# GDN's chunk chain: both scan directions in one operation, its scratch in step order, its output stored from ScalarE's queue

## The chip, the cores and the metric

The kernel runs on one core of one Trainium2 chip. The metric is the device time of one execution in microseconds (us), the median of the runs shown. The engines are named as the profile names them: PE (TensorE's matmuls; PEld is its weight load), DVE (VectorE), ACT (ScalarE), POOL (GpSimd) and SP (SyncE, which here only issues DMAs). Each engine works through its own instructions in order.

## The reference

One layer of a diffusion backbone over 2048 latent tokens with 256 context tokens in front and a model width of 1024: modulated RMS norms, one input projection split among three mixers (gated DeltaNet, RG-LRU, RWKV-7), one output projection, and a squared-ReLU MLP of width 4096. The mixers scan in both directions. The change is in the gated DeltaNet (GDN): 6 heads of width 64, chunks of 64 tokens, so 36 chunk steps in each direction, the context's 4 chunks first.

```python
# per direction and head, chunk by chunk (C = 64)
L    = strict_lower((k*beta) @ k.T * decay)
u, w = solve(L + I, [v*beta, k*beta*exp(gc)])
attn = (q @ k.T) * decay
def step(S, xs):
    v_new = u_c - w_c @ S
    o     = qg_c @ S + a_c @ v_new
    S     = S * exp(gl_c) + kd_c.T @ v_new
# forward and backward: context first, then the latents; the two outputs are added
```

## The kernel before

The program has four stages. The front projects RWKV's columns and prepares its features. `mixed` runs RWKV's chunk chain and, woven into it, `gdn_features`: GDN's projection, convolution and norms, and from them the scratch arrays in DRAM (`kq` for keys and queries, `kv` for keys and values by rows, `dm` for the decay matrices, `gc` for per-row factors). `rest` runs GDN's chunk chain and, woven into it, everything else before the MLP: the LRU's projection and scans, GDN's gate, and, behind them, the output projection `out_proj`. The MLP (`ffn`) comes last.

GDN's chain in `rest` has four parts, each written for one direction `dd` and called for both in turn:

- `gram(dd, n)` loads the keys and the decay matrix of a chunk, multiplies the decay by beta on POOL, forms three pairs of 64x64 Gram matrices on PE and writes the product into `mu` on DVE. Up to 32 such units fill a round.
- `Lanes.invert` inverts a round of 64x64 triangular matrices at once: 30 pairs of multiply and add on DVE, with transposes around them and small matmuls (`lmc`, `lmy`) behind. There are 7 rounds.
- `load(dd, n)` loads a chunk's operands, forms `q @ k.T` on PE and multiplies it by the decay (`qa`, two operations of 64 partitions on DVE), scales queries and keys by the row decays on POOL (`qa`, `kqe`) and the keys by rows on ACT (`kv`, three operations).
- `step(dd, n)` is the recurrence: PE, then `r` on DVE; PE, then `s<-gps,colt` (two halves) on DVE; PE, then the new state `s<-se,gps` (two halves) on DVE; then the output on PE, its copy on ACT and its store `go<-o` from SP's queue. POOL decays the old state (`se`) beside it.

`chains` writes them out step by step, with Gram matrices up to 10 steps ahead of the chain and loads one step ahead. `weave` gives the other work (`others`) a number of turns for each turn of the chain: 1.0 at first, 0.7 once `out_proj` has begun. A stage of `out_proj` may begin once the chain has passed the chunks that it reads; its first one waits for step 23 to be over. From the order in which it is written, a scheduler sets the order on each engine.

The DMAs that SP issues take turns on eight completion semaphores, so that an issue also stands until the DMA eight places before it has landed.

The lines of the steps below are L1267 (`gram`), L1284 (`load`), L1323 (`step`), L463 (`backwards`) and L1531 (`rest`).

Of the kernel before, what the change touches and what calls it, by code (L numbers as in the profile page):

```python
# [43 lines left out]
def poff(p):  # L44
# [10 lines left out]
    "kq": ([2, 128, NCH, 2, 3, 64], F32),  # L55
    "kv": ([2, 128, NCH, 2, 192], F32),
# [3 lines left out]
    "gc": ([128, NCH, 18], F32),  # L60
    "dm": ([2, 128, NCH, 3, 64], F32),
# [8 lines left out]
    "go": ([2, 128, NCH - 4, 3, 64], F32),  # L70
# [392 lines left out]
def backwards(k, rows, turn=False):  # L463


    if not turn:
        to, src = [rows(i).rearrange("(a t) c x -> a t (c x)", t=64) for i in (1, 0)]
        k.S.dma_start(out=to, in_=src[:, ::-1, :])
        return
    for c in range(4):  # L470
        to, src = [rows(i)[:, j].rearrange("(a t) x -> a t x", t=64) for i, j in ((1, 3 - c), (0, c))]
        k.S.dma_start(out=to, in_=src[:, ::-1, :])


def gdn_features(k, es, sm):
# [9 lines left out]
    def rows(p, y, a):  # L485
        to_rows(k, sm, w, d["kv"][0, :, 4 * p:4 * p + 4, a, :], y, "gsq")

    def normed(p, y, sq, s):

        scale = 64.0 if s else 1.0  # L490
        k.table("natural_log_exp_and_others")
        for a, b in ((0, 2), (2, 3)):
            ps = sm.tile([128, 2, 256], F32, name="gssq", tag="sm")
            for j in range(a, b):
                k.mm(ps[:, j - a, :], k.ones2, sq[:, j, :])
            k.act(sq[:, a:b, :], ps[:, 0:b - a, :], AF.Ln, scale=scale, bias=scale * 1e-6)
# [15 lines left out]
    for s, p, h in pj.passes([tiles(GW) + [(C_BA, 24)], tiles(0), tiles(2 * GW)]):  # L512
# [118 lines left out]
def gates(k):  # L631


    d, tc, V, A, G = k.d, k.tc, k.V, k.A, k.G
# [74 lines left out]
def decays(k, pp):  # L709
# [13 lines left out]
    for p in range(NP):  # L723
# [8 lines left out]
        cols = w.tile([128, 4, 18], F32, name="cols", bufs=2)  # L732
        for par in range(2):
            V.tensor_copy(cols[HALF[par]], ps[HALF[par], :, 32 * par:32 * par + 18])
        k.S.dma_start(out=d["gc"][:, 4 * p:4 * p + 4], in_=cols)
        yield
        for dd in range(2):
# [4 lines left out]
            col = cols[:, :, 3 * dd:3 * dd + 3].rearrange("p c r -> p r c")  # L742
# [6 lines left out]
            k.S.dma_start(out=d["dm"][dd, :, 4 * p:4 * p + 4], in_=e)  # L749
# [11 lines left out]
def rwkv_sweep(k, pj, pss, beside):  # L761
# [4 lines left out]
    with ExitStack() as es:  # L766
# [41 lines left out]
        for i, p in enumerate(RW_ORDER):  # L808
# [41 lines left out]
            backwards(k, vr, True)  # L850
# [242 lines left out]
def chunk_of(dd, n):  # L1093

    b, i = divmod(n, 4)
    return 4 * piece_of(dd, b) + (i if dd == 0 else 3 - i)


# [150 lines left out]
def gdn_mixer(k, es, ln):  # L1249
    rounds = Rounds([24] + 6 * [32])  # L1250
# [3 lines left out]
    colt = c1.tile([128, NCH, 18], F32, name="colt")  # L1254
# [4 lines left out]
    w = es.enter_context(tc.tile_pool(name="gmw", bufs=3, side="right"))  # L1259
    ch = es.enter_context(tc.tile_pool(name="gch", bufs=2, side="right"))  # L1260
# [5 lines left out]
    ee, late = {}, {}  # L1266

    def gram(dd, n):
        c = chunk_of(dd, n)
        kq = ld.tile([128, 3, 64], F32, name="kq")  # L1270
        dm = ld.tile([128, 3, 64], F32, name="dm", bufs=3)
        k.S.dma_start(out=kq, in_=d["kq"][dd, :, c, 0])
        k.S.dma_start(out=dm, in_=d["dm"][dd, :, c])
        k.tt(G, dm, dm, colt[:, c, 12 + 3 * dd:15 + 3 * dd].unsqueeze(2).to_broadcast([128, 3, 64]), MUL)
        ps = psg.tile([128, 3, 64], F32, name="gg")
        for r in range(3):
            for par in range(2):
                k.mm(ps[half[1 - par], r, :], kq[half[par], r, :], kq[half[par], r, :])
        for q, u, r, end in rounds.runs(6 * n + 3 * dd, 3):
            k.stt(mu[:, u, :], ps[:, r, :], -1.0, dm[:, r, :], MUL, MUL)  # L1280
            yield q if end else None

    def load(dd, n):
        c = chunk_of(dd, n)  # L1284
        sl = c % 2
        if n % 2 == 0:

            e = w.tile([128, 3, 128], F32, name="e")
            t = 128 * (c // 2)
            for par in range(2):  # L1290
                src = d["gb"][3, dd, par::2, t:t + 128].unsqueeze(0).to_broadcast([64, 3, 128])
                k.S.dma_start(out=e[half[par]], in_=src)
            ee[dd] = e
        e = ee[dd][:, :, 64 * sl:64 * sl + 64]
        kq = ld.tile([128, 2, 3, 64], F32, name="kqe", bufs=4)
        qa = ld.tile([128, 2, 3, 64], F32, name="qa", bufs=4)
        kv = ld.tile([128, 2, 3, 64], F32, name="kv", bufs=4)
        kn, vn = kv[:, 0], kv[:, 1]
        dm = ld.tile([128, 3, 64], F32, name="dml", bufs=2)
        k.S.dma_start(out=kq, in_=d["kq"][dd, :, c])  # L1300
        k.S.dma_start(out=dm, in_=d["dm"][dd, :, c])
        k.S.dma_start(out=kv, in_=d["kv"][dd, :, c].rearrange("p a (r x) -> p a r x", x=64))
        ps = psc.tile([128, 3, 64], F32, name="gps")
        for r in range(3):
            for par in range(2):
                k.mm(ps[half[1 - par], r, :], kq[half[par], 0, r, :], kq[half[par], 1, r, :])
# [5 lines left out]
        for r in range(3):  # L1312
            k.act(kn[:, r, :], kn[:, r, :], AF.Copy, scale=colt[:, c, 6 + 3 * dd + r:7 + 3 * dd + r])
        late[dd, n] = (kq, qa, vn, kn, e[:, :, 63:64])


    st = []
    for dd in range(2):
        s = ch.tile([128, 2, 3, 64], F32, name=f"s{dd}")
        G.memset(s, 0.0)  # L1320
        st.append(s)

    def step(dd, n):  # L1323
        kq, qa, vn, kn, el = late.pop((dd, n))
        c = chunk_of(dd, n)
        s, s2 = st[dd], ch.tile([128, 2, 3, 64], F32, name=f"s{dd}")
        st[dd] = s2
        z = psc.tile([128, 3, 64], F32, name="gps")
        for r in range(3):
            for par in range(2):  # L1330
                h, o = half[par], half[1 - par]
                k.mm(z[o, r, :], kq[h, 0, r, :], s[h, par, r, :])
        r_ = ch.tile([128, 3, 64], F32, name=f"r{dd}", bufs=1)
        k.tt(V, r_, vn, z, SUB)
        se = ch.tile([128, 3, 64], F32, name=f"se{dd}", bufs=1)
        for par in range(2):
            h = half[par]
            k.tt(G, se[h], s[h, par], el[h].to_broadcast([64, 3, 64]), MUL)
        yield
        v = psc.tile([128, 3, 64], F32, name="gps")  # L1340
        for r in range(3):
            for o in half:
                q, u = rounds.lane(dd, n, r)
                k.mm(v[o, r, :], ys[q % 2][o, u, :], r_[o, r, :])
        bt = colt[:, c, 12 + 3 * dd:15 + 3 * dd].unsqueeze(2).to_broadcast([128, 3, 64])
        for par in range(2):
            o = half[1 - par]
            k.tt(V, s[o, par], v[o], bt[o], MUL)
        yield
        ds = psc.tile([128, 3, 64], F32, name="gps")  # L1350
        for r in range(3):
            for par in range(2):
                h, o = half[par], half[1 - par]
                k.mm(ds[h, r, :], kn[o, r, :], s[o, par, r, :])
        for par in range(2):
            h = half[par]
            k.tt(V, s2[h, par], se[h], ds[h], ADD)
        yield
        if n >= 4:
            out = psl.tile([128, 3, 64], F32, name="gout", tag="lm")  # L1360
            for r in range(3):
                for par in range(2):
                    k.mm(out[half[par], r, :], s[:, par, r, :], qa[:, par, r, :])
            os = ch.tile([128, 3, 64], F32, name=f"o{dd}")
            A.copy(os[:, :, ::-1] if dd else os, out)
# [3 lines left out]
    def both(f):
        return lambda n: [f(dd, n) for dd in range(2)]  # L1370

    return chains(k, rounds, lambda n: chain(*both(gram)(n)), both(load), lambda q, m: ln.invert(mu, ys[q % 2], m, psl),
                  lambda n: zip(*both(step)(n)), 10, 1)


# [155 lines left out]
def rest(k, ln, rates=(1.0, 0.7)):  # L1531
# [44 lines left out]
def out_proj(k, es, wo):  # L1576
# [19 lines left out]
    def head(i):  # L1596
# [5 lines left out]
        z = m.tile([128, 3, 128], F32, name="oz")  # L1602
        o2 = go[:, 0].rearrange("p c r t -> p (c r t)").rearrange("p (r t) -> p r t", t=128)
        for dd in range(2):
            k.S.dma_start(out=go[:, dd], in_=d["go"][dd, :, t.start // 64:t.stop // 64])
# [256 lines left out]
```

## Time and profile before

| what | us |
| --- | --- |
| median of 3 runs (4234.94 to 4245.35) | 4235.84 |
| the profiled execution | 4235.04 |
| its span, first to last instruction | 4233.3 |
| `mixed`, about | 740 to 1790 of the span |
| GDN's chain, first to last `r` on DVE | 1848 to 2694 |
| MLP, from | about 2795 |

Busy shares over the whole span are 84% for PE, 55% for DVE, 35% for ACT and 34% for POOL. These are means over stages with different limits. The chain of waits at the end of the span runs through the MLP and stops at the end of `out_proj`, so it tells nothing of GDN's chain; that is read from stretches and from the rows of single operations.

### The profile page before, as it was taken

To read this page: it belongs to the slowest core of one execution; us is meant where nothing else is said; L and a number is where in the kernel's file an instruction comes from. 1 tells how busy PE (TensorE), PEld (TensorE's weight loads), DVE (VectorE), ACT (ScalarE), POOL (GpSimd) and SP (SyncE) were. 2 spreads that over 40 slices of the span, in tenths; PEclk is the share of its full clock that TensorE was granted. 3 is DMA by queue.
4 is the path that set the end of the run, shared out by engine and by line. 5 is a ranking of instruction groups with operands and counts; after the bars stand their busy time and mean duration, and the time that the engine had idled before them with its cause. 6 is when DMAs were issued, how large, how long until landed. Compare 5 with 4: busy or idle time off the path is not lost. (4 is left out here: it accounts for less than half of the span.)

```text
span 4233.3 us, 75399 instructions
## 1 busy us (share of the span) xinstructions
PE 3553.3 (84%) x29914; PEld 2971.8 (70%) x29914; DVE 2344.8 (55%) x4389; ACT 1487.1 (35%) x2987; POOL 1434.1 (34%) x1409
## 2 busy tenths in 40 slices
PE   3756689688969876778787689989999999999998
PEld 1645578577768765667665467768888887888886
DVE  2346467775785662349979985643333346333334
ACT  2344344343445433123445444532222223211212
POOL 3224222333334442124456644422322214222212
PEclk8868889688878887789888679999999999999999
DMA  8454434655666765375665455631122124111112
GB/s 206 103 142 124 125 110 143 213 151 153 195 189 193 234 183 173 107 243 157 188 193 177 152 180 172 215 112 53 57 62 66 50 70 132 51 49 45 50 45 85
DMA packets 568885, 566.06 MB, mean 134 GB/s; under 512 B 42180, under 2 KB 521045, under 8 KB 568533
## 3 DMA queue, kind: packets, MB, share of 16 engines
q1 hardware_dynamic: 554708, 538.16, 43.1%
q0 software_dynamic: 5120, 16.78, 1.4%
q10 hardware_dynamic: 8704, 6.29, 0.5%
q8 instruction: 237, 3.88, 0.4%
q14 instruction: 116, 0.94, 0.1%
HBM read 425.96 MB, written 145.77 MB: 135 GB/s over the span
## 5 line engine op out<-in xcount | busy, mean ns | idle before, releaser
L162 PE MATMUL proj<-hx,whi 128*128 128x258 f32 (+2 forms) x4080 | 859.5, 307 | 101.5 <-DMA hx<-ht 47.1
L162 PEld LDWEIGHTS proj<-hx,whi 128*128 128x128 f32 x4080 | 678.7, 201 | 145.3 <-issue 59.5
L162 PE MATMUL proj<-hx,wlo 128*128 128x258 f32 (+2 forms) x2040 | 611.8, 301 | 0.0
L136 DVE TENSOR_TENSOR facc<-facc,fdn 128x512 f32<-128x512 f32 x480 | 326.3, 687 | 399.0 <-PE fdn L162 399.0
L162 PEld LDWEIGHTS proj<-hx,wlo 128*128 128x128 f32 x2040 | 409.4, 201 | 10.1 <-issue 5.8
L162 PE MATMUL fup<-fhh,uhi 128*128 128x512 f32 x1024 | 404.9, 396 | 3.6 <-ACT fhh L344 3.6
L162 PE MATMUL fup<-fhl,uhi 128*128 128x512 f32 x1024 | 404.0, 395 | 3.3 <-DVE fhl L136 3.1
L162 PE MATMUL fup<-fhh,ulo 128*128 128x512 f32 x1024 | 403.7, 394 | 0.0
L162 PE MATMUL fdn<-dhi,ah 128*128 128x512 f32 x1024 | 399.4, 391 | 3.6 <-ACT ah L1762 1.7
L162 PE MATMUL fdn<-dlo,ah 128*128 128x512 f32 x1024 | 399.3, 390 | 0.0
L162 PE MATMUL fdn<-dhi,al 128*128 128x512 f32 x1024 | 395.2, 391 | 0.3 <-DVE al L136 0.3
L344 ACT CAST dhi<-draw 128x1024 fp32r<-128x1024 f32 x64 | 67.1, 1048 | 579.1 <-PE fdn L162 514.3
L136 POOL TENSOR_TENSOR dlo<-draw,dhi 128x1024 fp32r<-128x1024 f32 x32 | 77.5, 2422 | 563.2 <-ACT dhi L344 563.2
L136 POOL TENSOR_TENSOR fq<-fr 128x512 f32<-128x512 f32 x128 | 151.8, 1187 | 325.3 <-ACT fr L114 323.1
L162 PEld LDWEIGHTS fup<-fhl,uhi 128*128 128x128 f32 x1024 | 193.1, 189 | 49.0 <-DVE fhl L136 4.8
L162 PEld LDWEIGHTS fup<-fhh,uhi 128*128 128x128 f32 x1024 | 193.0, 189 | 48.7 <-ACT fhh L344 4.7
L162 PEld LDWEIGHTS fdn<-dhi,ah 128*128 128x128 f32 x1024 | 192.2, 188 | 47.6 <-DVE facc L136 3.0
L162 PEld LDWEIGHTS fup<-fhh,ulo 128*128 128x128 f32 x1024 | 193.0, 188 | 44.6
L162 PEld LDWEIGHTS fdn<-dhi,al 128*128 128x128 f32 x1024 | 192.2, 188 | 41.6 <-DVE al L136 0.8
L162 PEld LDWEIGHTS fdn<-dlo,ah 128*128 128x128 f32 x1024 | 192.3, 188 | 41.2
L136 DVE TENSOR_TENSOR al<-fq,ah 128x512 fp32r<-128x512 f32 x128 | 93.6, 732 | 227.7 <-ACT ah L1762 227.3
L144 DVE SCALAR_TENSOR_TENSOR gy<-proj,parB,gy 128x256 f32<-128x256 f32 x243 | 115.2, 479 | 160.9 <-ACT gy L114 149.4
(366 smaller groups left out, 7182.7 us busy)
## 6 DMA issues: line engine op xcount, KB each, us to landing
hx<-ht SPq DMA_DIRECT2D x144, 520.0 KB
hx<-ht SPq DMA_DIRECT2D x36, 1040.0 KB
uraw<-in_ffn_up_dram SPq DMA_DIRECT2D x64, 512.0 KB
draw<-in_ffn_down_dram SPq DMA_DIRECT2D x64, 512.0 KB
pk<-pk SPq DMA_DIRECT2D x18, 1536.0 KB
pk<-pk SPq DMA_DIRECT2D x36, 768.0 KB
ht<-mhh SPq DMA_DIRECT2D x36, 512.0 KB
pb<-pk SPq DMA_DIRECT2D x36, 384.0 KB
```

The lines of the kernel that those rows point to most:

```text
L136: return e.tensor_tensor(out=out, in0=a, in1=b, op=op)
L144: return self.V.scalar_tensor_tensor(out=out, in0=a, scalar=s, in1=b, op0=op0, op1=op1)
L162: self.last = self.PE.matmul(out, l, r, start=start, stop=stop).ins
L344: k.A.copy(hi, raw)
```

## The change

Both directions of a chunk step stand side by side in one tile: six units (two directions of three head pairs) where there were three. The scratch arrays `kq`, `kv`, `dm`, `gc` and `go` are laid out by step instead of by chunk and direction, so that one DMA brings both directions. For that, the features write the backward direction's chunks in reverse order, and `backwards` always copies chunk by chunk (four DMAs where there was one). The keys' row scaling goes from ACT (six operations for both directions) to POOL (one). The last step's new state is not formed. The output store goes from SP's queue to ACT's. Buffers are fewer: `kq` and `dm` of `gram` and `dml` of `load` have one buffer of double size each, where `dm` had three, `kq` two and `dml` two of single size. The rates of `weave` become 1.12 and 0.78.

```diff
-    "kq": ([2, 128, NCH, 2, 3, 64], F32),
-    "kv": ([2, 128, NCH, 2, 192], F32),
+    "kq": ([128, NCH, 2, 2, 3, 64], F32),
+    "kv": ([128, NCH, 2, 2, 192], F32),
...
-    if not turn:
-        to, src = [rows(i).rearrange("(a t) c x -> a t (c x)", t=64) for i in (1, 0)]
-        k.S.dma_start(out=to, in_=src[:, ::-1, :])
-        return
     for c in range(4):
         to, src = [rows(i)[:, j].rearrange("(a t) x -> a t x", t=64) for i, j in ((1, 3 - c), (0, c))]
         k.S.dma_start(out=to, in_=src[:, ::-1, :])
...
-    def gram(dd, n):
-        kq = ld.tile([128, 3, 64], F32, name="kq")
-        dm = ld.tile([128, 3, 64], F32, name="dm", bufs=3)
+    def gram(n):
+        kq = ld.tile([128, 2, 192], F32, name="kq", bufs=1)
+        dm = ld.tile([128, 6, 64], F32, name="dm", bufs=1)
+        k.S.dma_start(out=kq, in_=d["kq"][:, n, :, 0].rearrange("p e r t -> p e (r t)"))
+        k.S.dma_start(out=dm.rearrange("p u t -> p (u t)"), in_=d["dm"][:, n].rearrange("p e r t -> p (e r t)"))
+        k.tt(G, by2(dm), by2(dm), col(all_, n, 2), MUL)
...
-        dm = ld.tile([128, 3, 64], F32, name="dml", bufs=2)
+        dm = ld.tile([128, 6, 64], F32, name="dml", bufs=1)
...
-            k.tt(V, qa[o, par], ps[o], dm[o], MUL)
-            k.tt(G, qa[h, par], kq[h, 1], e[h], MUL)
-        k.tt(G, kq[:, 0], kq[:, 0], e, MUL)
-        for r in range(3):
-            k.act(kn[:, r, :], kn[:, r, :], AF.Copy, scale=colt[:, c, 6 + 3 * dd + r:7 + 3 * dd + r])
+            k.tt(V, qa[o, par], ps[o], dm[o], MUL)
+            k.tt(G, by2(qa[h, par]), kq[h, :, 1], e[h], MUL)
+        k.tt(G, kq[:, :, 0], kq[:, :, 0], e, MUL)
+        k.tt(G, kn, kn, col(all_, n, 1), MUL)
...
-        r_ = ch.tile([128, 3, 64], F32, name=f"r{dd}", bufs=1)
-        k.tt(V, r_, vn, z, SUB)
+        r_ = ch.tile([128, 6, 64], F32, name="r")
+        k.tt(V, by2(r_), vn, by2(z), SUB)
+        last = n + 1 == NCH
+        if not last:
...
-            k.S.dma_start(out=d["go"][dd, :, c - 4], in_=os)
+            A.dma_start(out=d["go"][:, :, n - 4].rearrange("p e r t -> p e (r t)"), in_=os.rearrange("p e r t -> p e (r t)"))
...
-def rest(k, ln, rates=(1.0, 0.7)):
+def rest(k, ln, rates=(1.12, 0.78)):
```

On DVE, in step 13 of the chain, where GDN's operations (`r`, `s`, `qa`, `mu`) stand among those of RWKV's output (`ro`) and GDN's gate (`zt`), before:

```order
L136 TENSOR_TENSOR r_21780<-kv,gps 128x192
L136 TENSOR_TENSOR ro_21539<-ro_21539,ro_21540 128x768
L141 TENSOR_SCALAR ro_21539<-ro_21539,parB 128x256 x3
L144 SCALAR_TENSOR_TENSOR zt<-zt,z 128x256
L136 TENSOR_TENSOR r_21793<-kv,gps 128x192
L136 TENSOR_TENSOR s_21408<-gps,colt 64x192 x2
L144 SCALAR_TENSOR_TENSOR mu<-gg,dm 128x192
L136 TENSOR_TENSOR s_21421<-gps,colt 64x192 x2
L144 SCALAR_TENSOR_TENSOR zt<-zt,z 128x256
L136 TENSOR_TENSOR qa<-gps,dml 64x192 x4
```

And on DVE in the same step now:

```order
L136 TENSOR_TENSOR r<-kv,gps 128x384
L136 TENSOR_TENSOR ro_20817<-ro_20817,ro_20818 128x768
L141 TENSOR_SCALAR ro_20817<-ro_20817,parB 128x256 x3
L144 SCALAR_TENSOR_TENSOR zt<-zt,z 128x256
L136 TENSOR_TENSOR s<-gps,colt 64x384 x2
L144 SCALAR_TENSOR_TENSOR zt<-zt,z 128x256
L136 TENSOR_TENSOR qa<-gps,dml 64x384 x2
L144 SCALAR_TENSOR_TENSOR zt<-zt,z 128x256
L136 TENSOR_TENSOR s<-se,gps 64x384 x2
```

Two instructions became one of double width throughout. From the first `r` of step 0 to the first of step 25 DVE has 1189 instructions before and 937 now: 200 fewer by this pairing, and 52 that now stand behind step 25, 36 of them of the last round's inversion (`ltmp`, `yl`, `x`).

On PE, where `out_proj`'s first matmuls (`opm`) stand between the chain's (`gps`) and those of a round's inversion (`lmc`, `lmy`), before:

```order
L162 MATMUL gps<-kqe 64x64 x3
L162 MATMUL ops<-ogo,ones_86 128x128 x3
L162 MATMUL gps<-kqe 64x64 x3
L162 MATMUL lmy<-y_16993,lc 32x32 x11
L162 MATMUL gps<-s_24790,kv 64x64 x6
L162 MATMUL ops<-ogo,ones_86 128x128 x3
L162 MATMUL gps<-s_24803,kv 64x64 x6
L162 MATMUL lmc<-x,mo 32x32 x16
L162 MATMUL opm<-ohi_23429,oh 128x512
```

And on PE at the first `opm` now:

```order
L162 MATMUL gps<-s,kqe 64x64 x5
L162 MATMUL ops<-ogo,ones_86 128x128 x3
L162 MATMUL gps<-s,kqe 64x64 x7
L162 MATMUL gout<-qa,s 64x64 x12
L162 MATMUL ops<-ogo,ones_86 128x128 x3
L162 MATMUL gps<-r,y_17046 64x64 x4
L162 MATMUL gps<-r,y_17047 64x64 x8
L162 MATMUL gps<-kqe 64x64 x8
L162 MATMUL opm<-ohi_22781,oh 128x512
```

The first `opm` moved from step 24 into step 25. Of the 768 `opm` matmuls 36 stand ahead of step 25's first matmul before and none now; when step 35 begins, 490 are done before and 444 now.

On SP, in the last third of `mixed`, where `backwards` (`kv<-kv`) stands between `gdn_features`' other DMAs and the next load of RWKV's chain (`pk<-pk`), before:

```order
L468 DMA kv<-kv 128x1x1536
L257 DMA adw_15153<-in_norm_mix_post_dram 128x128
L401 DMA hx<-ht 128x4x260
L256 DMA adw_15154<-in_ada_b_dram 128x128
L401 DMA hx<-ht 128x4x260 x3
L735 DMA gc<-cols 128x72
L1426 DMA pk<-pk 128x1536
```

And on SP at the same piece now:

```order
L468 DMA kv<-kv 128x1x384 x4
L750 DMA dm<-edm 128x4x192
L257 DMA adw_15189<-in_norm_mix_post_dram 128x128
L256 DMA adw_15190<-in_ada_b_dram 128x128
L742 DMA dm<-gb 64x3x256 x2
L401 DMA hx<-ht 128x4x260 x4
L736 DMA gc<-cols 128x4x9 x2
L1422 DMA pk<-pk 128x1536
```

Three more copies of `backwards` and one more store of `gc` now stand ahead of that load of `pk`.

## Rows read from the trace of the kernel before

**Rows 1.** Busy times by stretch: us; PE, PEld, DVE, ACT, POOL; clock, DMA

```profile
1790.00:1847.90 57.90, 23.05 (x210) 21.21 (x210) 8.22 (x16) 9.01 (x19) 19.99 (x30) 0.65 0.69 212
1847.90:2494.70 646.80, 502.66 (x6719) 415.90 (x6719) 580.73 (x1190) 280.40 (x591) 328.95 (x409) 0.82 0.60 183
2494.70:2693.60 198.90, 187.04 (x2017) 149.76 (x2019) 120.03 (x256) 93.41 (x259) 101.34 (x135) 0.93 0.58 177
2693.60:2795.00 101.40, 86.39 (x468) 68.50 (x462) 51.13 (x94) 51.99 (x130) 29.76 (x24) 0.94 0.57 180
...
1480.00:1790.00 310.00, 224.20 (x2973) 201.43 (x2971) 128.87 (x256) 94.19 (x192) 86.04 (x93) 0.79 0.52 154
```

**Rows 2.** DVE in order of time, steps 0, 25 and 35: start, us

```profile
1847.93 0.34 DVE L136 TENSOR_TENSOR r<-kv,gps 128x192 f32<-128x192 f32 x1
...
2494.73 0.35 DVE L136 TENSOR_TENSOR r<-kv,gps 128x192 f32<-128x192 f32 x1
...
2693.66 0.70 DVE L136 TENSOR_TENSOR r<-kv,gps 128x192 f32<-128x192 f32 x2 [0.56 <-PE gps L162]
```

**Rows 3.** DVE groups, 1847.9 to 2494.7: count | busy us, mean ns | idle before

```profile
L136 DVE TENSOR_TENSOR qa<-gps,dml 64x192 f32<-64x192 f32 x101 | 35.9, 355 | 2.2
L136 DVE TENSOR_TENSOR s<-gps,colt 64x192 f32<-64x192 f32 x100 | 35.5, 355 | 10.2 <-PE gps L162 7.7
L136 DVE TENSOR_TENSOR s<-se,gps 64x192 f32<-64x192 f32 x100 | 35.0, 350 | 4.8 <-PE gps L162 3.1
...
L144 DVE SCALAR_TENSOR_TENSOR mu<-gg,dm 128x192 f32<-128x192 f32 x62 | 21.6, 349 | 4.2 <-PE gg L162 3.8
...
L136 DVE TENSOR_TENSOR r<-kv,gps 128x192 f32<-128x192 f32 x50 | 17.2, 348 | 4.8 <-PE gps L162 4.3
```

**Rows 4.** DVE groups of RWKV's chain, 740 to 1790

```profile
L136 DVE TENSOR_TENSOR zl<-rkp,msk 64x384 f32<-64x384 f32 x72 | 40.0, 555 | 18.5 <-PE rkp L162 17.1
...
L136 DVE TENSOR_TENSOR am<-rbk,msk 128x384 f32<-128x384 f32 x72 | 37.2, 548 | 6.8 <-PE rbk L162 6.6
```

**Rows 5.** A tile's operations: duration ns min/median/max

```profile
L136 DVE TENSOR_TENSOR ltmp<-yl,ml x420: 144/376/1994, 801.5 to 2491.8; 128x30 f32<-128x30 f32 x14, 128x108 f32<-128x108 f32 x14, 128x168 f32<-128x168 f32 x14, 128x210 f32<-128x210 f32 x14
```

**Rows 6.** POOL and ACT groups, 1790 to 2713

```profile
L136 POOL TENSOR_TENSOR qa<-kqe,e 64x192 f32<-64x192 f32 x144 | 105.0, 729 | 21.5 <-PE gout L162 16.0
L136 POOL TENSOR_TENSOR se<-s,e 64x192 f32<-64x192 f32 x144 | 90.0, 625 | 54.2 <-DVE s L136 46.2 <-DMA e<-gb 1.7
L136 POOL TENSOR_TENSOR kqe<-kqe,e 128x192 f32<-128x192 f32 x72 | 46.7, 650 | 63.6 <-PE gps L162 61.5
...
L136 POOL TENSOR_TENSOR dm<-dm,colt 128x192 f32<-128x192 f32 x72 | 44.5, 622 | 168.4 <-DMA dm<-dm 138.0 <-DVE yl L136 11.3 <-DVE mu L144 5.9
...
L136 POOL TENSOR_TENSOR mx<-ogo 128x384 f32<-128x384 f32 x13 | 13.3, 1021 | 32.2 <-DVE ol L136 11.3 <-DMA ogo<-go 10.9 <-issue 8.7
...
L114 ACT ACTIVATE kv<-kv,colt 128x64 f32<-128x64 f32 x216 | 58.2, 337 | 81.6 <-DMA kv<-kv 75.5 <-PE gg L162 5.2 <-PE gps L162 0.9
```

**Rows 7.** POOL groups of RWKV's chain, 740 to 1790

```profile
L136 POOL TENSOR_TENSOR se<-sv,wend 64x384 f32<-64x384 f32 x72 | 63.0, 876 | 148.9 <-DVE sv L136 146.1
```

**Rows 8.** SP in order of time, one piece of `mixed`

```profile
1570.64 0.63 SPq L468 DMA_DIRECT2D kv<-kv  x1
...
1579.80 8.45 SPq L401 DMA_DIRECT2D hx<-ht  x3
1588.30 1.68 SPq L1426 DMA_DIRECT2D pk<-pk  x1
```

**Rows 9.** Waits by engine, 1480 to 1790: us, times, longest

```profile
POOL kw L136 <- DMA pk<-pk: 85.2, 9, 16.6
```

**Rows 10.** Waits of POOL and of SP's queue, 1847.9 to 2494.7

```profile
POOL dm L136 <- DMA dm<-dm: 110.6, 29, 13.3
...
SPq L1273 <- DVE mu L144: 36.5, 16, 8.2
SPq L1301 <- DVE qa L136: 22.6, 14, 6.0
```

More of the change, by code (lines that the diff above doesn't have):

```diff
@@ L460, in to_rows, with backwards @@
             k.S.dma_start(out=dst[HALF[1 - par], c::2, :], in_=n[HALF[c], par].rearrange("p b r x -> p b (r x)"))
[L463 to L469 removed]
+def backwards(k, rows):
     for c in range(4):
@@ L849, in rwkv_sweep @@
             to_rows(k, psn, w, vr(0), v, "c")
-            backwards(k, vr, True)
+            backwards(k, vr)
             kds = []
@@ L1265, in gdn_mixer @@
         G.memset(t, 0.0)
-    ee, late = {}, {}
-    def gram(dd, n):
-        c = chunk_of(dd, n)
-        kq = ld.tile([128, 3, 64], F32, name="kq")
-        dm = ld.tile([128, 3, 64], F32, name="dm", bufs=3)
[L1272 to L1275, printed above, removed]
-        for r in range(3):
[L1277 to L1280, printed above, removed]
+    late = {}
@@ new lines, in gdn_mixer @@
+    units = [(u, par) for u in range(6) for par in range(2)]
+    by2 = lambda t: t.rearrange("p (e r) t -> p e r t", r=3)
+    col = lambda h, n, a: colt[h, n, :, 3 * a:3 * a + 3].unsqueeze(3).to_broadcast([h.stop - h.start, 2, 3, 64])
+    all_ = slice(0, 128)
+    es_ = [None]
+    def gram(n):
[4 more added lines that the diff above has]
+        k.tt(G, by2(dm), by2(dm), col(all_, n, 2), MUL)
+        kq = kq.rearrange("p e (r t) -> p (e r) t", t=64)
+        ps = psg.tile([128, 6, 64], F32, name="gg")
+        for u, par in units:
+            k.mm(ps[half[1 - par], u, :], kq[half[par], u, :], kq[half[par], u, :])
+        for q, at, u, end in rounds.runs(6 * n, 6):
+            k.stt(mu[:, at, :], ps[:, u, :], -1.0, dm[:, u, :], MUL, MUL)
@@ L1346, in step @@
         for par in range(2):
             o = half[1 - par]
-            k.tt(V, s[o, par], v[o], bt[o], MUL)
+            k.tt(V, by2(s[o, par]), by2(v[o]), col(o, n, 2), MUL)
         yield
-        ds = psc.tile([128, 3, 64], F32, name="gps")
-        for r in range(3):
-            for par in range(2):
[L1353 to L1357, printed above, removed]
+        if not last:
+            ds = psc.tile([128, 6, 64], F32, name="gps")
+            for u, par in units:
+                dd, r = divmod(u, 3)
+                h, o = half[par], half[1 - par]
+                k.mm(ds[h, u, :], kn[o, dd, r, :], s[o, par, u, :])
+            for par in range(2):
+                h = half[par]
+                k.tt(V, s2[h, par], se[h], ds[h], ADD)
@@ L1358, in step @@
         yield
         if n >= 4:
[L1360 to L1365, printed above, removed]
-            k.S.dma_start(out=d["go"][dd, :, c - 4], in_=os)
+            out = psl.tile([128, 6, 64], F32, name="gout", tag="lm")
@@ L1367, in step @@
+            for u, par in units:
+                k.mm(out[half[par], u, :], s[:, par, u, :], qa[:, par, u, :])
+            os = ch.tile([128, 2, 3, 64], F32, name="o", bufs=2)
+            A.copy(os[:, 0], out[:, 0:3])
+            A.copy(os[:, 1, :, ::-1], out[:, 3:6])
+            A.dma_start(out=d["go"][:, :, n - 4].rearrange("p e r t -> p e (r t)"), in_=os.rearrange("p e r t -> p e (r t)"))
         yield
[L1369 to L1373, printed above, removed]
+    return chains(k, rounds, gram, load, lambda q, m: ln.invert(mu, ys[q % 2], m, psl), step, 10, 1)
@@ L1601, in head @@
         go = m.tile([128, 2, 2, 3, 64], F32, name="ogo")
-        z = m.tile([128, 3, 128], F32, name="oz")
+        z = m.tile([128, 3, 128], F32, name="oz", bufs=1)
         o2 = go[:, 0].rearrange("p c r t -> p (c r t)").rearrange("p (r t) -> p r t", t=128)
-        for dd in range(2):
-            k.S.dma_start(out=go[:, dd], in_=d["go"][dd, :, t.start // 64:t.stop // 64])
+        a, b = t.start // 64, t.stop // 64
+        for dd, src in enumerate((d["go"][:, 0, a:b], d["go"][:, 1, 32 - b:32 - a][:, ::-1])):
+            k.S.dma_start(out=go[:, dd].rearrange("p c r t -> p c (r t)"), in_=src.rearrange("p c r t -> p c (r t)"))
         for y, src in ((z, d["zs"]), (mx[:, 3:5, :], d["lo"]), (mx[:, 5:8, :], d["ro"])):
```

128 lines of the change are left out of this document (62 added, 66 removed).

## The prediction

> **What bounds the kernel now.** I read the busy times by stretch first, cut where GDN's chain begins, where its step 25 begins and where its step 35 begins. The cuts come from DVE's rows in order of time, which put `r` of steps 0, 25 and 35 at 1847.9, 2494.7 and 2693.7 [rows 2]. The reader is to see two limits in one chain. From step 0 to 25 DVE is busy 580.7 of 646.8 us (0.90) and PE 502.7 [rows 1]; DVE carries GDN's steps, the inversions, the LRU and RWKV's output, and sets the pace. From step 25 on, PE is busy 187.0 of 198.9 us and DVE only 120.0 [rows 1], because `out_proj` may then run; PE sets the pace there. Behind step 35 come 101.4 us of `out_proj` and the first products of the MLP [rows 1]. So a microsecond of DVE work taken out ahead of step 25 moves everything behind it, and one taken out later is mostly hidden by PE.
>
> **The change part by part.**
>
> *DVE, steps 0 to 24.* Before, a step has four `qa` at 355 ns, four `s<-gps` at 355, four `s<-se` at 350, two `mu` at 349 and two `r` at 348 [rows 3]: 1.42 + 1.42 + 1.40 + 0.70 + 0.70 = 5.63 us. Now it has two each of the first three with 64x384 elements and one each of the others with 128x384. RWKV's chain already has both forms on the same kinds of operands: 555 ns and 548 ns [rows 4]. That makes 6 x 0.555 + 2 x 0.548 = 4.43 us, 1.21 us less per step, and 30.2 us less in 25 steps. In the stretch that DVE bounds I take all of it: -30.2. If the idle share of 0.10 shrank with the work it would be 30.2 / 0.898 = -33.6; if the chain, not DVE, were late there, 0.
>
> *What moves behind step 25.* The order has 52 more DVE instructions behind that point than the pairing explains, most of them the last inversion, which only steps from 30 on need. At the mean of the stretch, 580.7 us over 1190 instructions or 0.49 us [rows 1], that is 25.4 us off DVE where it bounds and into the stretch where it is idle for 78.9 us of 198.9. Against this stand the 36 `opm` matmuls that were done ahead of step 25 and now come behind. The stretch from step 35 on took 101.4 us for 278 of them [rows 1], 0.365 us each with all that goes beside, so 13.1 us. Net -12.3; the ends are -28.3 (25.4 / 0.898, with the matmuls in PE's gaps) and 0 (the moved work is late where it is needed).
>
> *One chain instead of two.* Before, the two directions alternate, and one's matmuls run beside the other's DVE operation. Now DVE must find other work during twelve matmuls. No row shows this wait for GDN, so it is bounded by DVE's waits for the chain's matmuls in this stretch: 7.7 + 3.1 + 3.8 + 4.3 = 18.9 us [rows 3]. If they double, +18.9; if the neighbours cover them, as the order's rows between `r` and `s` suggest, 0. I take the middle, +9.5.
>
> *SP in `mixed`.* Each of nine pieces gets three more copies in `backwards`. One such issue took 0.63 us [rows 8], so 1.9 us per piece and 17 us in all. SP is in order, and RWKV's next load `pk<-pk` stands behind; POOL waited for that load 85.2 us in the last 310 us of the stage [rows 9], so this queue is not free there. The other small issues moved or added (one more store of `gc` per piece) are of the same kind. Between 0, where the load stands for a landing anyway (a group of `hx` loads ahead of it was issued over 8.45 us [rows 8]), and +17, I take a quarter, +4.
>
> *POOL and ACT.* `qa`, `se`, `kqe` and `dm` were 105.0 + 90.0 + 46.7 + 44.5 = 286.2 us [rows 6]. RWKV's `se` of twice the width costs 876 ns against 625 [rows 6, 7], a factor of 0.70 for two, so these become about 200 us. The keys' scaling that comes over from ACT is 36 operations of 128x384, at the 1021 ns of such an operation [rows 6] 36.8 us. POOL still loses 49 us, and ACT 216 operations and 58.2 us [rows 6]. Neither bounds a stretch, so I take 0; ACT's new store issues are 32, and ACT has 366 us free in the first stretch [rows 1]. The end without cover is the second rival.
>
> *A rule that speaks against the move to POOL.* Row first: the same DVE operation `ltmp`, whose two inputs are both in SBUF, took between 144 and 1994 ns [rows 5], far more than its sizes differ, and POOL's `qa` averages 729 ns where `se` of the same size averages 625 [rows 6]. The Trainium skill (SBUF — State Buffer, Who interferes with whom) says that a DVE instruction with two SBUF inputs and a GpSimd instruction that reads SBUF exclude each other for their whole length, while ScalarE waits for nobody. By that rule each scaling that leaves ACT for POOL can hold an inversion step on DVE; the rows agree that something of the kind happens, and since POOL's total falls, the sum by the rule is the same unless the new operations meet the inversions more often than the old.
>
> *The start, and from step 25 on.* Between 1790 and 1847.9 both DVE and PE mostly wait, with the DMA engines busy 0.69 of the time [rows 1]; the same bytes come in half as many loads, each from a single buffer. I take 0. Behind step 25 the DVE saving lies beside PE, with at best PE's idle 11.9 us to win [rows 1]; 0 as well.
>
> **The sum.** -30.2 - 12.3 + 9.5 + 4 = -29.0 us. The profiled execution took 4235.0 us (a span of 4233.3 and what lies around it), 0.8 below the median of the runs, so the forecast is 4206 us.
>
> **Rivals.**
>
> *More comes back.* DVE keeps its busy share and meets no new wait: -33.6 - 28.3 + 13.1 = -48.8, so 4186 us. For it: SP has half as many loads per step to place, and its loads `dm` and `dml` stood 36.5 and 22.6 us for DVE [rows 10]. Against it: less DVE work leaves less cover for the chain.
>
> *POOL holds DVE.* If each of the 25 new POOL operations ahead of step 25 stops DVE for its length, 25 x 1.021 = 25.5 us come back and the time is 4231. For it: the spread of `ltmp`; against it: the net fall of POOL's work. It is what the rule of the Trainium skill named above would make.
>
> *The small costs are all at their upper end.* The chain's waits double and SP delays RWKV's chain in every piece: -30.2 - 12.3 + 18.9 + 17 = -6.6, so 4228.
>
> *Single buffers hold the chain (slower).* `gram` now has one buffer for `dm`. Its load can leave SP only when DVE has written the previous `mu`, all loads of the chain queue behind it there, and POOL's multiplication stands for the landing with `se` and `kqe` behind it. POOL stood so 29 times for 110.6 us before, 3.8 us each [rows 10]. If half of the 25 steps now stop for that long and nothing covers it, 12.5 x 3.8 = 47.5 us come on top of the -29.0: 4253 us. It decides from about 1.2 us per step, where the gain is gone. Against it: Gram matrices run up to ten steps ahead of the chain, so a late one need not be missed.
>
> That the change does not do what it says is excluded by the order: every pair stands there as one operation.
>
> **How the numbers follow.** The forecast and what lies near it (4190 to 4223) has a chance of 0.60, more gain 0.17, POOL holding DVE 0.07, the small costs at their ends 0.07, the single buffers 0.09. A measurement of this kernel tells about 0.3% from no change, 12.7 us, so faster means below 4223: 0.60 + 0.17 = 0.77. Within 0.3% are the two middle rivals, 0.14; slower is the last, 0.09. The range goes from 4168, between the first rival and the sum of all lower ends (-33.6 - 28.3 - 11.9, 4161), to 4230, which leaves out the last rival and about half of POOL's.
>
> **What would show it.** In the changed profile the operations `s`, `qa` and `r` should average 0.55 us with half the counts, and step 25's `r` should begin some 30 to 45 us earlier than 2494.7, if `mixed` ends at the same place. From step 25's `r` to step 35's should take 199 us as before within 10, and the rest about 13 us more. The forecast is wrong if DVE's busy share ahead of step 25 falls below 0.86, if `dm<-dm` stops POOL for more than the 110.6 us of before, or if RWKV's chain ends more than 10 us later.

## The result and the profile after

The changed kernel took 4279.67 us (median; 4276.09 to 4290.47), the kernel before 4238.17 beside it: a ratio of 1.010, interval 1.0076 to 1.0123. It is slower by some 41 us, where 29 less were forecast, and outside the range.

The trace is read in two parts, with marks that do not depend on the order in which GDN's steps were put: the start of the last `rout` matmul of RWKV's chain ends `mixed`, that of the last `opm<-ohi,oh` ends the stage `rest`. Before they stand at 1789.7 and 2779.5, after at 1823.6 and 2825.4. So `mixed` is 33.9 us longer, `rest` 12.0 us longer, and what is behind 0.7: together the 46.6 by which the span grew, 4233.3 to 4279.9.

Busy times of the changed kernel by stretch, in the columns of [rows 1]: the start, steps 0 to 24, steps 25 to 34, from step 35 to the last `opm`, and the last part of `mixed`:

```profile
1823.60:1876.70 53.10, 15.91 (x182) 14.29 (x176) 7.37 (x12) 6.59 (x10) 21.26 (x24) 0.58 0.72 214
...
1876.70:2519.40 642.70, 478.75 (x6694) 405.14 (x6694) 555.82 (x937) 233.14 (x417) 293.95 (x260) 0.82 0.59 179
2519.40:2723.90 204.50, 185.38 (x2028) 146.12 (x2028) 132.88 (x217) 83.96 (x212) 110.98 (x105) 0.94 0.59 179
2723.90:2825.40 101.50, 95.19 (x468) 75.93 (x469) 52.80 (x85) 49.95 (x127) 29.39 (x22) 0.97 0.60 186
...
1480.00:1790.00 310.00, 206.06 (x2614) 185.41 (x2612) 118.13 (x243) 87.39 (x176) 80.31 (x87) 0.73 0.55 154
```

DVE's instructions ahead of step 25 fell from 1190 to 937, as the order said, but its busy time only from 580.7 to 555.8 and the stretch from 646.8 to 642.7. In the same 310 us of `mixed`, PE was busy 206 us instead of 224.

DVE's GDN groups in steps 0 to 24 of the changed kernel, as in [rows 3]:

```profile
L136 DVE TENSOR_TENSOR s<-gps,colt 64x384 f32<-64x384 f32 x50 | 27.8, 555 | 12.0 <-PE gps L162 10.6
L136 DVE TENSOR_TENSOR qa<-gps,dml 64x384 f32<-64x384 f32 x50 | 27.8, 555 | 2.6 <-PE gps L162 1.5
L136 DVE TENSOR_TENSOR s<-se,gps 64x384 f32<-64x384 f32 x50 | 27.4, 548 | 1.1
...
L144 DVE SCALAR_TENSOR_TENSOR mu<-gg,dm 128x384 f32<-128x384 f32 x29 | 16.0, 550 | 17.4 <-PE gg L162 15.6 <-POOL se L136 1.3 <-issue 0.2
L136 DVE TENSOR_TENSOR r<-kv,gps 128x384 f32<-128x384 f32 x25 | 13.8, 551 | 13.0 <-PE gps L162 8.4 <-DMA e<-gb 4.2
```

The paired operations take what RWKV's took, 548 to 555 ns. The DVE work that was to go is gone; the time is not.

**Where `mixed` lost.** SP's queue in order of time, one piece of the changed kernel, to be held against [rows 8]:

```profile
1631.81 2.56 SPq L460 DMA_DIRECT2D kv<-rows  x4
1635.17 8.62 SPq L468 DMA_DIRECT2D kv<-kv  x4
1643.83 3.80 SPq L750 DMA_DIRECT2D dm<-edm  x1
...
1652.27 4.14 SPq L401 DMA_DIRECT2D hx<-ht  x4
1656.50 3.43 SPq L736 DMA_DIRECT2D gc<-cols  x2
1660.02 1.79 SPq L1422 DMA_DIRECT2D pk<-pk  x1
```

Four copies of 192 KB hold SP for 8.62 us (5.8 to 8.6 in the pieces that begin ahead of the chain's end) where one copy of 768 KB took 0.63. RWKV's last `pk<-pk` was issued at 1739.8 before and at 1777.6 after. POOL's waits for these loads did not grow in all, though: before (1480 to 1790) they were the 85.2 us of [rows 9] and 15.3 ahead of another operation, after (1480 to 1824) 99.3. What grew is POOL's wait for `gp<-adw`, a store that SP issues for other work woven into `mixed` (the modulation weights `adw`), and ACT's wait for the next load of these weights, which POOL issues behind it. Before, and then after:

```profile
POOL adw L242 <- DMA pk<-pk: 15.3, 1, 15.3
POOL adw L242 <- DMA gp<-adw: 14.4, 4, 6.8
...
POOL kw L136 <- DMA pk<-pk: 99.3, 10, 16.4
POOL adw L242 <- DMA gp<-adw: 35.2, 3, 13.8
```

ACT's wait for `adw<-in_ada_w_dram` went from 29.5 to 57.1 us. From 1480 to the end of `mixed` these two waits are 26 to 35 and 57 to 65 us in the four kernels whose four copies go out from SP (the change, experiments 2, 3 and 4), and 0.5 to 14 and 0 to 30 in three where they do not (before, experiments 1 and 7). How much of the delay each wait makes was not separated.

**Where `rest` lost.** DVE and POOL in order of time in the changed kernel (start, us, instruction):

```profile
2306.52 1.13 DVE L136 TENSOR_TENSOR s<-se,gps 64x384 f32<-64x384 f32 x2
2307.68 0.30 DVE L136 TENSOR_TENSOR ltmp<-yl,ml 128x130 f32<-128x130 f32 x1
2307.73 1.92 POOL L136 TENSOR_TENSOR se<-s,e 64x384 f32<-64x384 f32 x2 [2.12 <-DVE s L136]
...
2308.87 0.93 DVE L136 TENSOR_TENSOR yl<-yl,ltmp 128x130 f32<-128x130 f32 x1
2309.73 0.83 POOL L136 TENSOR_TENSOR kv<-kv,colt 128x384 f32<-128x384 f32 x1
2309.84 0.90 DVE L136 TENSOR_TENSOR ltmp<-yl,ml 128x150 f32<-128x150 f32 x1
2310.52 1.35 POOL L136 TENSOR_TENSOR li<-li,xc 128x512 f32<-128x512 f32 x1
2310.77 1.27 DVE L136 TENSOR_TENSOR yl<-yl,ltmp 128x150 f32<-128x150 f32 x1
```

Add start and length: `yl` ends at 2309.80, POOL's two `se` at 2309.65; `ltmp` at 2310.74, POOL's `kv` at 2310.56; `yl` at 2312.04, POOL's `li` at 2311.87. All three times a DVE operation with both inputs in SBUF lasts until POOL's has ended; the `ltmp` that began ahead of `se` took 0.30. Operations with an input in PSUM keep their length (the `s` of 555 and 548 ns above). I call *hold* the sum, over DVE's operations without a PSUM input from the last `rout` to the last `opm`, of duration less the shortest of the same operation and form there in any of these traces. It was 119.8 us before and 150.4 after, 31 more. All but 13 and 14 us of it lies in operations that overlap one of POOL's, though POOL is busy less than half of the stage.

The Trainium skill (SBUF — State Buffer, Who interferes with whom) says that a DVE instruction with two SBUF inputs and a GpSimd instruction that reads SBUF exclude each other. The trace agrees: the three ends above lie 0.15 to 0.18 us behind POOL's.

POOL's GDN groups of the changed kernel over `rest`, beside [rows 6]:

```profile
L136 POOL TENSOR_TENSOR qa<-kqe,e 64x384 f32<-64x384 f32 x72 | 81.4, 1131 | 68.4 <-PE gout L162 65.6 <-DMA kqe<-kq 0.2
L136 POOL TENSOR_TENSOR se<-s,e 64x384 f32<-64x384 f32 x70 | 67.8, 969 | 30.8 <-DVE s L136 27.7
L136 POOL TENSOR_TENSOR kqe<-kqe,e 128x384 f32<-128x384 f32 x36 | 39.4, 1095 | 79.2 <-PE gps L162 78.7 <-DMA kqe<-kq 0.3
L136 POOL TENSOR_TENSOR kv<-kv,colt 128x384 f32<-128x384 f32 x36 | 35.6, 989 | 18.7 <-DMA kv<-kv 15.1 <-DMA ogo<-go 2.2
```

There are half as many and they take less in all, but each is half as long again: `qa` 1131 against 729 ns, `se` 969 against 625. That a longer operation holds more is the theory; the experiments must show it.

### The profile page after: what moved, and what is told of

Same layout as the page of the kernel before. It is cut to its first block, busy times and chain, and to the rows that moved or that the text cites. A ratio compares the mean times of both kernels' runs of the same rounds, so it can differ in the third digit from the quotient of the medians.

```text
span 4279.9 us, 74064 instructions
## 1 busy us (share of the span) xinstructions
PE 3535.6 (83%) x29890; PEld 2965.1 (69%) x29890; DVE 2336.0 (55%) x4117; ACT 1432.5 (33%) x2771; POOL 1409.6 (33%) x1226
```

## The experiments

Where nothing else is said, an edit is made to the changed kernel. "Stage" is the time from the last `rout` to the last `opm`, "idle" the stage less DVE's busy time. Before: stage 989.8, hold 120, idle 235. After: 1001.8, 150, 253. What single traces can tell: the change and experiments 2 and 3 have the same order of work in `mixed`, and it ended at 1823.6, 1804.4 and 1814.1. In `rest` no two kernels have the same order, since the scheduler sets it anew with every edit: the kernel before and experiment 4 differ in `mixed` alone, and yet only 934 of DVE's 1540 instructions in the stage match in order, and it took 989.8 and 978.8. Differences below some 20 us in the one and 11 in the other are read from medians alone.

**1. `kv` by chunk.** The old layout of `kv`, so one copy per piece and two loads per step.

```
-    "kv": ([128, NCH, 2, 2, 192], F32),
+    "kv": ([2, 128, NCH, 2, 192], F32),
-            backwards(k, lambda i: d["kv"][:, steps_of(i, p), i]...)      # four copies
+            backwards(k, lambda i: d["kv"][i, :, 4 * p:4 * p + 4]...)     # one copy
```

> The changed kernel with kv alone back in its old layout: backwards is one DMA per piece again, and the chain loads kv in two DMAs per step instead of one. If the four copies per piece hold SP's queue in mixed (they were issued over about 8 us per piece where the one copy took 0.63), the chain's first r comes back from 1876.7 to about 1850 us and the whole to about 4253 us. If the loss in mixed is of the smaller stores of gc and dm or of another order of instructions, the first r stays at 1870 to 1880 and the time at about 4280. The stretch from r of step 0 to r of step 25 should stay near 643 us in both.

4227.26 us, ratio to before 0.9995 (0.9983 to 1.0007). The last `rout` came at 1771.0 instead of 1823.6, and the time fell by 26 us more than was expected. The stage stayed long, 1003.6, with hold 154. So more than the whole loss in `mixed` goes with `kv`'s way to DRAM, and the saving in `rest` is missing for another reason.

**2. The keys scaled on ScalarE.** POOL's one operation per step becomes six on ScalarE, as before.

```
-        k.tt(G, kn, kn, col(all_, n, 1), MUL)
+        for u in range(6):
+            dd, r = divmod(u, 3)
+            k.act(kn[:, dd, r, :], kn[:, dd, r, :], AF.Copy, scale=colt[:, n, dd, 3 + r:4 + r])
```

> The changed kernel with the keys' row scaling back on ACT (six operations of 128x64 per step instead of one of 128x384 on POOL). If the new POOL operation lengthens DVE's operations that read two SBUF tensors, DVE's busy time from r of step 0 to r of step 25 falls from 556 to about 530 us, POOL's by 24 us, the stretch from 643 to about 620 us, and the time to about 4258. If the wider POOL operations as such, or the single chain's waits, take the gain, DVE's busy time stays within 8 us of 556 and the time within 8 us of 4280. The first r stays at about 1877.

4269.74 us, 1.0088 (1.0068 to 1.0108), hardly under the 1.010 of the change and between the two values expected. The stage took 1007.2, idle was 263 and the hold 147. POOL was busy 413 us in the stage instead of 456, and DVE was held about as long.

**3. The old rates.** `rates=(1.0, 0.7)` in `rest`.

> The changed kernel with weave's rates back at 1.0 and 0.7. If the new rates crowd the chain with other work ahead of step 24 (the chain waits for DVE behind it), the stretch from r of step 0 to r of step 25 shortens by 10 to 25 us, paid back in part behind step 35. If the rates only make up for the chain's fewer turns, less of the other work is done by step 25, the end behind step 35 gets longer and the time is 4280 to 4310 us.

4267.61 us, 1.0074 (1.0052 to 1.0097). Step 0 to step 25 took 589.7 instead of 642.7, yet the stage 999.9: the mark at step 25 moves with the order and the end does not. (In experiment 4, whose code in `rest` is that of the kernel before, the same stretch took 610.7 instead of 646.8.)

**4. The kernel before with four copies.**

```
-            backwards(k, lambda i: d["kv"][i, :, 4 * p:4 * p + 4].rearrange("p c a x -> p c (a x)"))
+            for c in range(4):
+                to, src = [d["kv"][i, :, 4 * p + c].rearrange("(a t) b x -> a t (b x)", t=64) for i in (1, 0)]
+                k.S.dma_start(out=to, in_=src[:, ::-1, :])
```

> The kernel before with one part of the change alone: backwards copies kv chunk by chunk, four DMAs per piece (27 more in all), layouts and everything else as before. If these copies hold SP's queue in mixed, the first r moves from 1848 to about 1875 us and the time from 4238 to about 4265. If the loss in mixed comes from the smaller stores or the new order, the first r stays within 6 us of 1848 and the time within 8 us of 4238.

4247.62 us, 1.0032 (1.0019 to 1.0046): 14 us slower by the ratio, 17 by the medians. In the trace the last `rout` came 27 us later, as was expected, but the stage was 11 shorter, so that the time stayed under the expected 4265. SP's queue in it:

```profile
1496.09 8.38 SPq L543 DMA_DIRECT2D kv<-kv  x4
```

The copies alone, without the pairing, hold SP as long.

**5. Two buffers for `dml`** (on experiment 1; `o` has one in exchange): `name="dml", bufs=2` and `name="o"` with one.

> The kernel of the first experiment (kv by chunk, one copy per piece) with two buffers for dml instead of one, and one instead of two for o to make room. Theory single buffers: in the first experiment DVE stood once for 21.3 us for the first dml, and SP stood some 80 us behind DVE's last use of dml, with the loads of the gate behind it; with two buffers SP no longer stands there, ScalarE's wait for zs falls from 47 towards the 14 us of the kernel before, and the time falls by 10 to 20 us against 4227. Rival, POOL holds DVE: the excess of DVE's SBUF operations stays at about 149 us and the time within 5 us of 4227. Rival, o with one buffer costs what dml gives: same time, with ScalarE waiting for the store of o.

4237.12 us, 1.0013 (1.0003 to 1.0023): 10 slower than experiment 1, where 10 to 20 less were expected. Idle fell by 7 to 246, and the hold rose by 13 to 167. Whether `o` or the new order did that isn't settled; more buffers did not bring the gain back.

**6. Without POOL's products by the decay** (on experiment 1, with the keys on ScalarE).

```
-            k.tt(G, by2(qa[h, par]), kq[h, :, 1], e[h], MUL)
-        k.tt(G, kq[:, :, 0], kq[:, :, 0], e, MUL)
+            A.copy(by2(qa[h, par]), kq[h, :, 1])
```

> The kernel of the first experiment, with the scalings by the decay left out: POOL's products of kqe and qa with e are gone (qa's half is copied by ScalarE), and the keys are scaled on ScalarE as in the kernel before. Left out is the multiplication of queries and keys by the decay. Theory POOL holds DVE: these three groups held DVE's operations 24.3, 11.2 and 10.3 us; the excess of DVE's SBUF operations in the rest falls from 149 to about 105 us, DVE's busy time by some 40 us, and the time by 20 to 40 us. Rival, chain and transfers pace the rest, not DVE's busy time: the excess falls as much, but DVE's idle time grows by it and the time stays within 8 us of 4227. Rival, what holds DVE is not POOL: the excess stays at 140 to 150.

4184.4 us, 0.9888 (0.9871 to 0.9905), 43 under experiment 1. The hold fell by 44 to 110, the stage by 49 to 954.8, and idle (249) did not grow. Against experiment 12, which has the keys on ScalarE too, hold and stage both fall by 40 and the median by 38. DVE with its hold does set the pace. (The profiled execution was 12 us under the median, so its trace may show the falls too large by up to that.)

**7. The four copies from ScalarE's queue.**

```
-        k.S.dma_start(out=to, in_=src[:, ::-1, :])
+        (q or k.S).dma_start(out=to, in_=src[:, ::-1, :])     # q is k.A for kv
```

> The changed kernel with the four copies of kv per piece issued from ScalarE's queue instead of SP's. Theory SP's order: SP is held 8.2 to 8.4 us per piece while it issues the four copies, and the loads of RWKV's chain and of hx stand behind; freed of them RWKV's chain ends near 1775 to 1795 instead of 1818 and the time falls by 20 to 40 us from 4280, less what ScalarE loses by standing there (up to 8 us per piece). Rival, the transfers themselves: the copies keep the loads waiting wherever they are issued, and the time stays within 8 us of 4280. Rival, ScalarE is now the one held, slower than 4285.

4234.24 us, 1.0008 (0.9995 to 1.0021), where the change has 1.010: some 39 us come back, with the same copies in the same layout. The last `rout` came at 1779.1. ScalarE was held instead, here by the third and fourth copy of a piece, and the time fell even so:

```profile
1488.41 10.00 ACTq L468 DMA_DIRECT2D kv<-kv  x2
```

So it was the place in SP's order, not the traffic: POOL's wait for `gp<-adw` is 7.4 us here.

**8. Experiment 5 with the keys on ScalarE.**

> The fifth experiment with the keys scaled on ScalarE again. If POOL holding DVE and the single buffer both cost time, this is the fastest so far: 10 us under the first experiment by the buffer and 5 to 10 us by the 10 us that kv held DVE, about 4210. If the second experiment's end to end gain of 10 us came from elsewhere, it stands with the fifth.

4243.7 us, 1.0031 (1.0019 to 1.0044), stage 1013.8, hold 153. The expectation failed. Against experiment 5 the hold fell by 14, but idle grew by 19 to 265; which wait that is was not followed. Less hold is worth something only where DVE is not made to wait instead.

**9. POOL's operations split** (on experiment 1). `dm`, `qa`, `kqe`, the keys and `se` each as two operations, one direction each; DVE's stay paired. For `qa`, and so for the others:

```
-            k.tt(G, by2(qa[h, par]), kq[h, :, 1], e[h], MUL)
+            for dd in range(2):
+                k.tt(G, by2(qa[h, par])[:, dd], kq[h, dd, 1], e[h, dd], MUL)
```

> The first experiment with every one of POOL's GDN operations split in two, one direction each (dm, qa, kqe, the keys, se), and DVE's left paired. Same products, twice the POOL operations of half the size. Theory length of POOL's operations: a DVE operation on SBUF that meets one waits for its end, so the hold goes with the square of the length; of the 76 us held by qa, se, kqe, kv and dm about 25 come back (55 of 76, as the kernel before had 49 without kv), the excess falls from 149 to about 125 us and the time by 10 to 25 us from 4227, though POOL's total rises by some 50 us. Rival, POOL's total decides: the excess stays or grows and the time is 4225 to 4245. Rival, POOL's operations are on the chain (se), slower: above 4240.

4219.3 us, 0.9970 (0.9960 to 0.9980), 8 under experiment 1 by the medians, where 10 to 25 were expected. POOL was busy 506 us in the stage instead of 448; the hold fell from 154 to 142, not to 125, and the stage to 997.9. More POOL time and less hold: total is not what decides. But a hold of 144 stands in experiment 7 too, whose operations are long, so this experiment alone does not tell length from order.

**10. Split, with the keys on ScalarE.** Experiments 9 and 2 together, on experiment 1.

> The ninth experiment with the keys scaled on ScalarE again, so POOL does the same products in the same sizes as before the change. Theory length of POOL's operations: the excess comes back to the 116 to 128 us of the kernel before, and the time is 4227 less about 30, 4190 to 4212. Rival, POOL's total: 4220 to 4240.

4195.97 us, 0.9924 (0.9908 to 0.9940): faster than both kernels. Its stretch from the last `rout` to the last `opm`, in the columns of [rows 1]:

```profile
1775.90:2749.10 973.20, 769.84 (x9372) 636.75 (x9369) 718.18 (x1250) 423.81 (x979) 464.07 (x589) 0.84 0.61 187
```

**11. The kernel before without POOL's products by the decay**, as in experiment 6.

> The kernel before, with the products of kqe and qa with the decay left out as in the sixth experiment (qa's half is copied by ScalarE). Left out is the multiplication of queries and keys by the decay. It asks what the pairing on DVE is worth where POOL holds less. Theory POOL ate the gain: qa and kqe held DVE about 23 us before, so this stands about 15 to 25 us under the kernel before, and the sixth experiment (4184) is 15 to 35 us faster than this one. Rival, the pairing is worth nothing in any case (the chain paces): this one is as fast as the sixth, 4175 to 4190.

4203.59 us, 0.9939 (0.9923 to 0.9955). Its stage:

```profile
1788.90:2751.10 962.20, 782.07 (x9396) 639.12 (x9393) 731.43 (x1541) 474.29 (x1124) 325.65 (x378) 0.87 0.62 190
```

and that of experiment 6:

```profile
1761.30:2716.10 954.80, 755.36 (x9374) 627.91 (x9369) 705.85 (x1251) 456.65 (x1052) 297.57 (x267) 0.86 0.62 191
```

With little hold on either side the pairing takes 25.6 us off DVE (731.4 to 705.9), but the stage shrinks by 7.4, less than single traces can tell: idle grows from 231 to 249. The medians lie 19 us apart, the two traces 34, and 27.6 of these are the earlier end of `mixed` (1761.3 against 1788.9).

**12. Experiment 1 with the keys on ScalarE.** Its edit differs from that of experiment 10 by the length of POOL's operations alone.

> The first experiment with the keys scaled on ScalarE again. In the second experiment this edit went with 10 us less at the end but no shorter rest. Theory POOL holds DVE: the keys' operations held 10.3 us, so 4217 to 4225. Rival, the order that the other operations fall into decides more than this: 4225 to 4245, as in the eighth.

4222.29 us, 0.9975 (0.9965 to 0.9986). Its stage:

```profile
1776.40:2771.00 994.60, 767.20 (x9370) 635.31 (x9366) 745.39 (x1251) 424.71 (x980) 420.47 (x375) 0.85 0.60 183
```

From 12 to 10, POOL's busy time rises by 44 us (420.5 to 464.1), the hold falls from 150 to 122, DVE's busy time by 27, the stage by 21 and the median by 26. POOL's groups of experiment 10 have the length of before:

```profile
L136 POOL TENSOR_TENSOR qa<-kqe,e 64x192 f32<-64x192 f32 x144 | 95.7, 683 | 68.6 <-PE gout L162 48.3 <-DMA kqe<-kq 17.8
L136 POOL TENSOR_TENSOR se<-s,e 64x192 f32<-64x192 f32 x140 | 84.0, 618 | 77.3 <-DVE s L136 74.0
```

The rival is the order, which is new in each kernel (926 of DVE's 1250 instructions match in order between 10 and 12). What order does beside long operations can be seen in the change and experiments 1, 2, 3, 5, 7, 8 and 12: hold 144 to 167, stage 995 to 1014. Experiment 10 lies outside both. And if each lengthening of a DVE operation is put down to the POOL operation that it overlaps most, the hold per microsecond of that operation falls into two groups by length, whatever the order:

| POOL's operation | long, both directions in one | short, one direction |
| --- | --- | --- |
| `qa` | 0.27 to 0.35 (8 traces) | 0.17 to 0.21 (4) |
| `se` | 0.31 to 0.41 (9) | 0.20 to 0.24 (5) |
| `dm` | 0.32 to 0.41 (9) | 0.20 to 0.26 (5) |

Together these show the length of POOL's operations as what raised the hold.

What pairing on DVE is worth in `rest` by itself is not shown. The stage of experiment 10 is 16.6 us shorter than that of the kernel before and 5.6 shorter than experiment 4's, whose code there is the same as before; 13.8 us of its lead come from the earlier end of `mixed`.

## Why the prediction was wrong, point by point

Of its three signs of being wrong, the last came true: RWKV's chain ended 33.9 us later, while DVE's share ahead of step 25 was 0.865 and POOL's wait for `dm` fell.

*DVE, steps 0 to 24: right in durations.* The five groups shown, with 2.8 us of `mu` in smaller forms, are 115.6 us against 147.1 (the 145.2 of [rows 3] and 1.9 of smaller forms), 31.5 less where 30.2 was said. In busy time it is less: neighbouring DVE instructions overlap in the profile, by 45.7 us before and 34.7 after in this stretch, and busy time counts an overlap once.

*SP in `mixed`: the step that failed.* Its price was 0.63 us for each copy more, and a quarter of 17 us was taken, +4. Measured: +33.9 at the end of `mixed`, twice the upper end. The four copies take some 7 us more of SP per piece, not 1.9: the first two of a piece take 0.61 to 0.69 us each, but the third, where it follows at once, 1.1 to 3.1 and the fourth 3.8 to 5.1. The third and fourth of the piece shown above:

```profile
1637.54 1.07 SPq L468 DMA_DIRECT2D kv<-kv  x1
...
1638.65 5.13 SPq L468 DMA_DIRECT2D kv<-kv  x1
```

The wait that grew is not the one it named either (POOL for `pk<-pk`) but the one for `gp<-adw`. The least, median and largest of the changed kernel's copies (ns) hide the pattern in the median,

```profile
L468 SPq DMA_DIRECT2D kv<-kv x36: 584/666/5135, 1500.1 to 1849.0; - x36
```

and the trace of before had it in a row that the prediction did not look up, RWKV's own copies of this form:

```profile
L472 SPq DMA_DIRECT2D vr<-vr x36: 596/688/4005, 143.1 to 757.2; - x36
```

Where four of these stood in a row they were issued in 4.8 to 8.1 us; the row of a single larger copy was the wrong one.

*POOL and ACT, "I take 0": the second step that failed.* It weighed POOL's total, which fell as said (286.2 to 256.0, a little less than forecast), and so let POOL pass as off the path. The hold grew by 31 us, and with that most of the paired saving was spent: over the whole stage the durations of GDN's own DVE operations fell by 45.0 (203.6 to 158.6), DVE's busy time by 5.9. The rival "POOL holds DVE" named the mechanism, but tied it to the new operations alone and priced it at 25.5. Experiments 2 and 12, without the new ones, have a hold of 147 and 150: they are not the point. 10 against 12 and the table there show that the length is.

*One chain instead of two: not where it was looked for.* +9.5 of 0 to 18.9 was taken. By the prediction's own measure, DVE's waits for `gps` and `gg` in steps 0 to 24, it is 36.1 us in the rows above, near a doubling; but 15.6 of them is one wait for `gg`, which stood ahead of step 0 in the kernel before (24.2). Over the whole stage these waits fell, `gps` from 35.7 to 29.1 and `gg` from 34.4 to 15.8. DVE's waits before,

```profile
DVE mu L144 <- PE gg L162: 34.4, 7, 24.2
...
DVE s L136 <- PE gps L162: 18.8, 15, 2.5
...
DVE qa L136 <- PE gps L162: 10.3, 7, 5.3
...
DVE r L136 <- PE gps L162: 6.6, 11, 1.5
...
DVE ox L140 <- DMA x<-ox: 3.8, 3, 2.7
```

and after:

```profile
DVE qa L136 <- DMA dml<-dm: 22.1, 1, 22.1
DVE ox L140 <- DMA x<-ox: 19.3, 7, 5.2
...
DVE mu L144 <- PE gg L162: 15.8, 2, 15.6
...
DVE r L136 <- PE gps L162: 13.8, 8, 5.2
DVE s L136 <- PE gps L162: 13.8, 7, 4.1
```

Idle as a whole grew by 17.9, and it is 246 to 265 us in the eleven paired kernels and 216 to 235 in the three unpaired ones. The largest rises are the one wait for the first `dml` and the waits for `out_proj`'s `x`. In the first 140 us of the stage DVE was busy as long as before (74.8 and 73.1), so the start took no more. What makes idle longer was not separated; DVE's waits for the chain's matmuls do not show it.

*What moves behind step 25: not a gain.* The 52 instructions moved, but the next ten steps grew to 204.5 from 198.9 and `opm` started later. Over the whole stage the same work is done; counting -12.3 rested on a mark that moves with the order, as experiment 3 shows.

*Single buffers hold the chain: not so.* POOL's wait for `dm` in steps 0 to 24 fell from the 110.6 of [rows 10]:

```profile
POOL dm L136 <- DMA dm<-dm: 88.7, 19, 12.4
```

SP did stand longer for the single `dml` (its lines L1303 against L1301 before),

```profile
SPq L1303 <- DVE qa L136: 41.1, 13, 8.6
...
SPq L1303 <- DVE ltmp L136: 30.0, 5, 11.4
```

but a second buffer (experiment 5) gave no time.

With what was measured the sum closes: +33.9 in `mixed`; in `rest` -45.0 of GDN's durations, +30.6 of hold, +9.5 because DVE's fewer instructions overlap less (44.6 us instead of 54.1), -1.0 of the rest, +17.9 of idle; +0.7 behind: 46.6, which is what the span grew by.

## What to carry to other kernels

When two operations are put into one, ask of each engine that shares SBUF with another not only what it does in all but how long one of its operations lasts, and leave them short on the engine that holds the one that is the bound. What pairing is worth on the bound itself is to be read in its busy time and the stage, not in the sum of its durations. Price a DMA that an in-order queue must issue by the row where the same copies already stand one behind the other, and by what is queued behind them. Measure a stage between marks that the order cannot move.

## What the runs showed of the hardware

A copy of 768 KB within DRAM was issued in 0.63 us, the same bytes as four copies in 5.8 to 8.7 on SP, and two of them held ScalarE for 10.00. In each piece it is the fourth that is held, and the third where it follows at once. Why was not tried.

The hold on DVE per microsecond of POOL differed by the operations' length: `qa` held DVE 19 us for 105 us of POOL before, and 24 for 81 after; `kqe` 5 for 47 and 12 for 39.

Left open: the paired kernels in which SP issues no four copies of `kv` end `mixed` between 1761 and 1779, ahead of the 1789.7 of before; what in the new layouts gives that was not tried.
